# The first y_b product issued inside attention's last round

## The chip, the cores and the metric

The kernel runs on one core of a Trainium2 chip. The metric is the device time of one execution in microseconds (us); three executions of a kernel give a median. A core has TensorE (PE, with its weight loads shown apart as PEld), VectorE (DVE), ScalarE (ACT), GpSimd (POOL), and SyncE (SP), which here only issues DMA transfers, in order. Each engine works through its own list of instructions in order; between engines there are semaphores.

## The reference, cut to what matters

The reference is one decoder block on 2048 positions and a width of 1024, in float32. One projection feeds two branches: dilated band attention (three head groups of eight heads, 64 wide) and a gated linear recurrence (RG-LRU). The two results are gated, added, projected and normalised:

```python
attn = attn.reshape(B, S, ATTN_OUT_WIDTH).astype(dt) * jax.nn.silu(g_attn)
y_a = attn @ w_attn_proj[l]
...
y_b = (h * jax.nn.silu(g_lru)) @ w_lru_proj[l]
gates = jax.nn.sigmoid(gate_logits).reshape(B, S, N_BRANCHES, D)
merged = gates[:, :, 0] * y_a + gates[:, :, 1] * y_b
out = merged @ w_out[l] + b_out[l]
x = layer_norm(DEEPNORM_ALPHA * x + out, ln_gain[l], ln_bias[l])
```

The product for y_b needs the recurrence alone, not the attention. It is computed transposed: 8 blocks of 128 output channels by 4 chunks of 512 positions, 32 blocks in all, each a sum over 8 blocks of 128 channels.

## The kernel before, in words

The program has three stages in a row. The projection and the recurrence come first (the `q` products of line 602). Attention follows, and then the back end: the y_b jobs, the combination of the head groups, the y_a jobs and the output projection with its normalisation. Every float32 operand of a large product is split in a high part and a rest, so that one product is three matmuls (high by high, high by rest, rest by high).

**Attention** is written as a software pipeline of 48 units of work, `i` from 0 to 47, with three more turns of the loop to empty it. In turn `i` the loop issues the scores of `i` (line 981, into PSUM tiles with the tag `s`, four of them, one bank each), masks and maximum of `i` on DVE (line 988), exponentials of `i` and `i - 1` on ACT (line 996), the transposes of the exponentials of `i - 1` in two halves (`turn(i - 1, 0)` and `turn(i - 1, 1)`, line 1006, 16 small matmuls each in these units, into PSUM tiles with the tag `t`), the copies of those transposes to SBUF (`bring`, lines 1019 and 1021), and the product with the values of `i - 2` (`values`, line 1034, which also takes a `t` tile, `o`). Three turns later `leave` copies `o` to SBUF on DVE (lines 1043 to 1047), and a turn after that SP stores it to DRAM. There are four `t` tiles, used in rotation: a half of a unit's transposes takes two, a value product takes one. Turn 48 issues the transposes of unit 47 and the values of unit 46; turn 49 the values of unit 47.

The operands of y_b are made during attention: `prep_wl` loads and splits two 128-column weight blocks at a time (`wl`), `load_h` the recurrence's output of the first chunk (`h`), split by POOL. After the loop `prep_wl(4)` to `prep_wl(7)` put eight more weight loads on SP's queue, behind the last stores of attention's outputs (`o_scr<-ot`) and of its statistics (`st_scr<-sta`).

**The y_b jobs**, `yb_job(n)` for n from 0 to 31, follow. Each takes one of four PSUM tiles with the tag `y`, issues 24 matmuls (lines 1281 to 1283), and has DVE multiply the result with the gate `gB` (line 1287), which `load_gb` has fetched from DRAM; SP stores it to `yb_scr` (line 1288). Job n asks for the gate of job n + 2. The pools of attention are closed before those of the back end are opened, so the `y` tiles lie in banks that were `s` tiles. Job 1 also reads attention's statistics back (`stats`), from which DVE and ACT work out the groups' weights (lines 1184 to 1200); a transpose inside job 6 (line 1208) uses them. Splits of the weights for jobs 4 to 7 stand between these on ACT (line 1072) and DVE (line 1073).

The order of each engine's list is the order in which the code below is written; nothing moves it later.

Of the kernel before, what the change touches and what calls it, by code (L numbers as in the profile page):

```python
# [8 lines left out]
F32 = mybir.dt.float32  # L9
F32R = mybir.dt.float32r  # L10
AF = mybir.ActivationFunctionType
ALU = mybir.AluOpType
# [3 lines left out]
P = 128  # L16
S = 2048
D = 1024
KT = 8
NCH = 4  # L20
CH = 512
# [10 lines left out]
def hybrid_block_kernel(ctx: ExitStack, tc: tile.TileContext, a: dict, out: bass.AP):  # L32
    nc = tc.nc
    sp, act, dve, pool, pe = nc.sync, nc.scalar, nc.vector, nc.gpsimd, nc.tensor
# [12 lines left out]
    mg_scr = dram.tile([2 * D, S], F32, name="mg_scr")  # L47
    yb_scr = dram.tile([D, S], F32, name="yb_scr")
# [40 lines left out]
    now = {"n": 0}  # L89
# [831 lines left out]
    n = len(where)  # L921
# [61 lines left out]
    def peak(i, j, h):  # L983
        u, q = divmod(i, 4)
        lo = first(i, j)
        if h == 0:
            st["p", i, j] = p_p.tile([P, 2, 256], F32, tag="p", name=f"p{i}{j}")
        dve.tensor_tensor_reduce(out=st["p", i, j][:, h, lo:256], in0=st["s", i, j // 2][h][:, j % 2, lo:256],  # L988
                                 in1=mask[:, lo:256], scale=1.0, scalar=3e38, op0=ALU.add, op1=ALU.min,
                                 accum_out=sta[u][:, 4 * q + j, h:h + 1])  # L990
# [32 lines left out]
    def values(i):  # L1023
        u, q = divmod(i, 4)
        g, hp = unit(u)
        V = VT[g, hp // 2]
        o = st["o", i] = aps.tile([P, 4, P], F32, tag="t", name=f"o{i}", bufs=4)
        for j in range(4):
            ptb = st["b", i, j // 2]
            n = 4 * q + j  # L1030
            for x in range(first(i, j) // P, 2):
                for h, hs in enumerate(HALF):
                    v0 = P * (hp % 2) + 64 * h
                    pe.matmul(o[hs, j, :], V[:, n if x else prev(g, n), v0:v0 + 64], ptb[:, j % 2, x, h, :],  # L1034
                              start=(x == first(i, j) // P), stop=(x == 1))
# [48 lines left out]
    def load_h(c, k, lag):  # L1084
# [3 lines left out]
        sp.dma_start(flat(t[:, 1]), hb_scr[k * P:(k + 1) * P, c * CH:(c + 1) * CH])  # L1088
        later(lag, lambda: split(t[:, 0], t[:, 1], dve if c else pool))

    NG = 48
    for fn in v_parts(2, 0) + third:
        fn()
# [2 lines left out]
    for i in range(NG + 3):  # L1096
        u = i // 4
        on, turns = i < NG, 0 < i <= NG
        run(late)
        if i in VORD:  # L1100
            loads += v_parts(*VORD[i])
        if i % 4 == 0 and 1 <= u <= 9:
            loads += unit_parts(u + 2)
        for _ in range(2):
            if loads:
                loads.pop(0)()
        if on:
            scores(i)
        if i > 2:
            leave(i - 3)  # L1110
        if turns:
            expo(i - 1, 2, 1)
            expo(i - 1, 3, 0)
            expo(i - 1, 3, 1)
        if on:
            peak(i, 0, 0)
            expo(i, 0, 0)
            for j, h in ((0, 1), (1, 0), (1, 1)):
                peak(i, j, h)
        if turns:  # L1120
            turn(i - 1, 0)
            bring(i - 1, 0, 0, act)
            bring(i - 1, 0, 1, dve)
        if on:
            for j, h in ((0, 1), (1, 0), (1, 1)):
                expo(i, j, h)
            peak(i, 2, 0)
            peak(i, 2, 1)
        if turns:
            turn(i - 1, 1)  # L1130
            light = unit((i - 1) // 4)[0] == 2 or i % 3 == 0
            bring(i - 1, 1, 0, dve if light else act)
        if on:
            peak(i, 3, 0)
            peak(i, 3, 1)
            expo(i, 2, 0)
        if turns:
            bring(i - 1, 1, 1, dve)
        if i > 1 and i - 2 < NG:
            values(i - 2)  # L1140
        if i in (40, 41):
            prep_wl(i - 40, 2)
        if 42 <= i < 46:
            load_h(0, 2 * (i - 42), 2)
            load_h(0, 2 * (i - 42) + 1, 2)
        if i in (46, 47):
            prep_wl(i - 44, 2)
        now["n"] += 1
# [118 lines left out]
    def load_gb(n):  # L1267
        c, f = divmod(n, 8)
        GB[n] = gt(f"gB{n}")
        sp.dma_start(GB[n], mg_scr[D + f * P:D + (f + 1) * P, c * CH:(c + 1) * CH])  # L1270

    def yb_job(n):
        c, f = divmod(n, 8)
        cs = slice(c * CH, (c + 1) * CH)
        run(late)
        if n + 2 < 32:
            load_gb(n + 2)
        yb = fp.tile([P, CH], F32, tag="y", name=f"yb{c}{f}", bufs=4)
        for k in range(8):
            xx = HH[c, k]  # L1280
            pe.matmul(yb, WL[f][:, 0, k], xx[:, 0], start=(k == 0), stop=False)  # L1281
            pe.matmul(yb, WL[f][:, 0, k], xx[:, 1], start=False, stop=False)  # L1282
            pe.matmul(yb, WL[f][:, 1, k], xx[:, 0], start=False, stop=(k == 7))  # L1283
            if k == 3:
                run(pe_late)
        gb = GB.pop(n)
        dve.scalar_tensor_tensor(out=gb, in0=gb, scalar=1.0, in1=yb, op0=ALU.add, op1=ALU.mult)
        later(1, lambda: sp.dma_start(yb_scr[f * P:(f + 1) * P, cs], gb))
        now["n"] += 1
# [7 lines left out]
        sp.dma_start(YG[i][0], mg_scr[f * P:(f + 1) * P, cs])  # L1297
        sp.dma_start(YG[i][1], yb_scr[f * P:(f + 1) * P, cs])

    load_gb(0)  # L1300
    load_gb(1)
    for n in range(32):
        c, f = divmod(n, 8)
# [223 lines left out]
```

## Time and profile before

| | us |
|---|---|
| median of 3 executions (lowest to highest) | 2129.75 (2129.43 to 2129.99) |
| the profiled execution's own time | 2130.19 |
| its span, first to last instruction | 2128.4 |
| turn 48 of attention begins on PE (first transposes of unit 47) | at 1663.35 |
| first y_b matmul | at 1669.35 |
| second y_b job begins | at 1674.94 |

The granted TensorE clock is 0.998 of full speed over the span. PE is busy for 98% of the span. The times in the last three rows are counted from the span's start. A row of the timeline gives the start, the duration, the engine, the line, the operation with its output and input, and in square brackets how long the engine had stood idle before it and who ended that idle time. PE's end of a matmul is modelled, so neighbouring matmuls overlap in the rows; what one costs in a stream is the distance between starts.

### The profile page before, as it was taken

The numbers are of one execution on the slowest core, as the hardware profiler recorded it, in microseconds if no ns is written. First come the engines' busy times: TensorE is split into PE (matmuls) and PEld (weight loads), VectorE is DVE, ScalarE is ACT, GpSimd is POOL, SyncE is SP. The second block draws the span as 40 slices with busy tenths as digits, with TensorE's granted clock in tenths as the row PEclk, the third lists the DMA queues.
The fourth block names the chain that finished last, engine by engine and source line by source line (L and its number), as shares of the span: only waits on it lengthen the run. The fifth ranks groups of instructions, "written<-read, shape, count | busy, mean of one in ns | idle before, by whom it ended". The sixth has DMA issues, their size and how long they took to land.

```text
span 2128.4 us, 35700 instructions
## 1 busy us (share of the span) xinstructions
PE 2093.8 (98%) x12016; PEld 1745.9 (82%) x12016; DVE 1672.6 (79%) x3193; ACT 1078.8 (51%) x2284; POOL 457.6 (22%) x397
## 2 busy tenths in 40 slices
PE   8999999999999999999999999999999999999998
PEld 7888888888878888888888888888888888878887
DVE  8888889799789867787787887886999645476667
ACT  6355445357356566546557656657999411121100
POOL 1001011011011002121221221223535444332120
PEclk9999999999999999999999999999999999999999
DMA  9987997988988876677778788879998688874431
GB/s 273 275 267 218 290 261 238 272 265 250 278 271 257 305 220 196 221 226 219 249 251 270 262 256 254 256 227 383 289 310 262 210 280 281 290 246 162 163 109 70
DMA packets 348263, 525.72 MB, mean 247 GB/s; under 512 B 123568, under 2 KB 156336, under 8 KB 344240
## 3 DMA queue, kind: packets, MB, share of 16 engines
q1 hardware_dynamic: 330368, 491.64, 71.3%
q0 software_dynamic: 10080, 18.35, 5.4%
q10 hardware_dynamic: 7632, 13.44, 1.7%
q8 instruction: 96, 1.57, 0.3%
q14 instruction: 87, 0.71, 0.1%
HBM read 318.18 MB, written 190.45 MB: 239 GB/s over the span
## 4 chain that ended last, share of the span: by engine, by line
PE 60%; ACT 6%; DMA 3%; DVE 2%; issue 1%; SPq 1%; POOL 0%; DVEq 0%; ACTq 0%
PE q L602 37%; ACT p L996 4%; PE z L1393 3%; PE z L1391 3%; PE z L1392 3%; PE yb L1281 2%; PE yb L1282 2%; PE yb L1283 2%; PE o L1034 1%; ACT ptb L1019 1%; PE ya L1361 1%; PE ya L1360 1%; PE ya L1359 1%; PE s L981 1%; DMA yb_scr<-gB 1%; DVE p L988 1%
## 5 line engine op out<-in xcount | busy, mean ns | idle before, releaser
L602 PE MATMUL q<-xT,hS 128*128 128x512 f32 x1680 | 518.8, 390 | 0.0
L602 PE MATMUL q<-xT,l 128*128 128x512 f32 x1120 | 436.0, 389 | 0.0
L602 PE MATMUL q<-xB,hA 128*128 128x512 f32 x1248 | 387.3, 392 | 5.7 <-ACT xB L207 5.7
L602 PEld LDWEIGHTS q<-xT,hS 128*128 128x128 f32 x1680 | 314.1, 188 | 64.3
L602 PE MATMUL q<-xB,l 128*128 128x512 f32 x904 | 352.9, 390 | 0.5 <-DMA l<-wl_scr 0.4
L602 PEld LDWEIGHTS q<-xB,hA 128*128 128x128 f32 x1248 | 234.1, 188 | 54.4 <-ACT xB L207 5.7
L602 PEld LDWEIGHTS q<-xT,l 128*128 128x128 f32 x1120 | 210.2, 188 | 44.3
L602 PEld LDWEIGHTS q<-xB,l 128*128 128x128 f32 x904 | 170.1, 188 | 37.5 <-DMA l<-wl_scr 0.8
L264 ACT ACTIVATE hA<-wA 128x512 fp32r<-128x512 f32 x218 | 135.5, 623 | 82.1 <-DMA wA<-in_w_in_dram 44.0
L602 PE MATMUL q<-xB,hS 128*128 128x512 f32 x560 | 173.5, 391 | 2.2 <-DVE v L219 2.2
L996 ACT ACTIVATE p<-p,sta 128x256 f32<-128x256 f32 (+1 forms) x384 | 172.2, 455 | 5.9 <-DVE sta L988 5.2
L602 PE MATMUL q<-xT,hA 128*128 128x512 f32 x560 | 172.8, 390 | 0.0
L237 POOL DMA_DIRECT2D wS<-in_w_in_dram x70 | 61.1, 935 | 477.6 <-DMA wS<-in_w_in_dram 120.0
L264 ACT ACTIVATE hS<-S 128x512 fp32r<-128x512 f32 x175 | 109.0, 623 | 87.9 <-DVE S L219 48.4
L219 POOL TENSOR_TENSOR S<-S,wA 128x512 f32<-128x512 f32 x35 | 45.6, 1303 | 445.8 <-DVE S L219 319.1
L602 PEld LDWEIGHTS q<-xB,hS 128*128 128x128 f32 x560 | 104.2, 188 | 23.8 <-issue 2.6
L602 PEld LDWEIGHTS q<-xT,hA 128*128 128x128 f32 x560 | 104.7, 188 | 21.9 <-issue 0.4
L988 DVE CUSTOM_DVE_ANT_0 p<-s,mask 128x256 f32<-128x256 f32 (+1 forms) x384 | 118.8, 360 | 4.6 <-PE s L981 3.6
L1393 PE MATMUL z<-wo,ml 128*128 128x512 f32 (+1 forms) x264 | 101.1, 383 | 0.8 <-DVE ml L1378 0.8
L1391 PE MATMUL z<-wo,mh 128*128 128x512 f32 (+1 forms) x264 | 101.1, 383 | 0.1
L1392 PE MATMUL z<-wo,mh 128*128 128x512 f32 (+1 forms) x264 | 101.0, 383 | 0.0
L1281 PE MATMUL yb<-h,wl 128*128 128x512 f32 x256 | 100.3, 392 | 0.0
(199 smaller groups left out, 4182.1 us busy)
## 6 DMA issues: line engine op xcount, KB each, us to landing
wA<-in_w_in_dram SPq DMA_DIRECT2D x253, 256.0 KB, 5.0
wl_scr<-l SPq DMA_DIRECT2D x105, 512.0 KB, 5.3
l<-wl_scr SPq DMA_DIRECT2D x105, 512.0 KB, 4.8
sw<-y SPq DMA_DIRECT2D x384, 64.0 KB, 3.1
wS<-in_w_in_dram SPq DMA_DIRECT2D x70, 256.0 KB, 4.8
wS<-in_w_in_dram POOLq DMA_DIRECT2D x70, 256.0 KB, 6.4
qh_scr<-hi SPq DMA_DIRECT2D x48, 256.0 KB, 5.8
v_scr<-vs SPq DMA_DIRECT2D x48, 256.0 KB, 4.4
```

The source lines that it names most:

```text
L219: eng.tensor_tensor(out=out, in0=in0, in1=in1, op=op)
L237: pool.dma_start(t, w_part(s, x), accum_op=ALU.add)
L264: act.activation(h, r, AF.Copy)
L602: pe.matmul(bank, w[:, ks], x[:, kk, xx], start=(first and i == 0), stop=(last and i == 11))
L988: dve.tensor_tensor_reduce(out=st["p", i, j][:, h, lo:256], in0=st["s", i, j // 2][h][:, j % 2, lo:256], in1=mask[:, lo:256], scale=1.0, s ...
L996: act.activation(p, p, AF.Exp, scale=-1.0, bias=s[:, h:h + 1], accum_out=s[:, 2 + h:3 + h])
L1281: pe.matmul(yb, WL[f][:, 0, k], xx[:, 0], start=(k == 0), stop=False)
L1282: pe.matmul(yb, WL[f][:, 0, k], xx[:, 1], start=False, stop=False)
L1283: pe.matmul(yb, WL[f][:, 1, k], xx[:, 0], start=False, stop=(k == 7))
L1391: pe.matmul(z, mh[:, k], w[:, 0, hs], start=(k == 0), stop=False)
L1392: pe.matmul(z, mh[:, k], w[:, 1, hs], start=False, stop=False)
L1393: pe.matmul(z, ml[:, k], w[:, 0, hs], start=False, stop=(k == 7))
```

## The change

The 24 matmuls of the first y_b job move into turns 48 and 49 of the attention loop, with a fourth user of the tag `s` as their PSUM tile. The values of unit 46 move ahead of the second half of the transposes of unit 47. The gate for this job is fetched in turn 48, into a tile of the pool `p_p` that held exponentials, and the multiplication and the store to `yb_scr` are issued in turn 50. `yb_job(0)` keeps what else it did (`run(late)`, the load of the gate for job 2) and returns; `load_gb(0)` goes.

```diff
+    Y0 = {}
+
+    def yb_first(k0, k1):
+
+        if k0 == 0:
+            Y0["b"] = aps.tile([P, 2, 256], F32, tag="s", name="yb00", bufs=4).rearrange("p a b -> p (a b)")
+        for k in range(k0, k1):
+            xx = HH[0, k]
+            pe.matmul(Y0["b"], WL[0][:, 0, k], xx[:, 0], start=(k == 0), stop=False)
+            pe.matmul(Y0["b"], WL[0][:, 0, k], xx[:, 1], start=False, stop=False)
+            pe.matmul(Y0["b"], WL[0][:, 1, k], xx[:, 0], start=False, stop=(k == 7))
+
+    def yb_first_gate():
+        g = Y0["g"] = p_p.tile([P, 2, 256], F32, tag="p", name="gB0").rearrange("p a b -> p (a b)")
+        sp.dma_start(g, mg_scr[D:D + P, 0:CH])
+
+    def yb_first_out():
+        g = Y0["g"]
+        dve.scalar_tensor_tensor(out=g, in0=g, scalar=1.0, in1=Y0["b"], op0=ALU.add, op1=ALU.mult)
+        sp.dma_start(yb_scr[0:P, 0:CH], g)
+
...
+        if i == NG:
+            values(i - 2)
+            yb_first(0, 2)
         if turns:
             turn(i - 1, 1)
...
             bring(i - 1, 1, 1, dve)
-        if i > 1 and i - 2 < NG:
+        if i == NG:
+            yb_first_gate()
+            yb_first(2, 4)
+        if i > 1 and i != NG and i - 2 < NG:
             values(i - 2)
+        if i == NG + 1:
+            yb_first(4, 8)
+        if i == NG + 2:
+            yb_first_out()
...
         if n + 2 < 32:
             load_gb(n + 2)
+        if n == 0:
+            now["n"] += 1
+            return
...
-    load_gb(0)
     load_gb(1)
```

What this makes of the engines' lists is shown at two places. The first is PE at the end of attention. In the names `pt470` and `pt471` are the two halves of unit 47's transposes (a last digit tells the two tiles of a half), `o46` and `o47` the value products, `yb00` and `yb01` the first two y_b jobs; what a row waits for stands in brackets, and a line of dots stands for rows of the same kind. Before:

```order
L1006 MATMUL pt4701_19249<-ident_180,p471_19165 128x64
L1006 MATMUL pt4710_19269<-ident_180,p472_19192 128x64 [waits DVE_49,Activation_49]
...
L1006 MATMUL pt4711_19270<-ident_180,p473_19215 128x64
L1034 MATMUL o46_19290<-ptb460_19186,V11_16983 64x128 [waits DVE_49]
L1034 MATMUL o46_19290<-ptb461_19213,V11_16983 64x128 x8
L1034 MATMUL o47_19313<-ptb470_19266,V11_16983 64x128 [waits Activation_49]
L1034 MATMUL o47_19313<-ptb471_19287,V11_16983 64x128 [waits DVE_49]
L1281 MATMUL yb00_19375<-h00_18738,wl0_18551 128x512 [waits Pool_49]
...
L1281 MATMUL yb01_19416<-h00_18738,wl0_18551 128x512
```

Changed, at the same place:

```order
L1006 MATMUL pt4701_19249<-ident_180,p471_19165 128x64
L1034 MATMUL o46_19269<-ptb460_19186,V11_16983 64x128 [waits DVE_49]
L1034 MATMUL o46_19269<-ptb461_19213,V11_16983 64x128 x8
L1099 MATMUL yb00_19286<-h00_18738,wl0_18551 128x512 [waits Pool_49]
...
L1006 MATMUL pt4710_19293<-ident_180,p472_19192 128x64 [waits DVE_49,Activation_49]
...
L1099 MATMUL yb00_19286<-h00_18738,wl0_18551 128x512 [waits Pool_49]
...
L1034 MATMUL o47_19328<-ptb470_19266,V11_16983 64x128 [waits Activation_49]
L1034 MATMUL o47_19328<-ptb471_19311,V11_16983 64x128 [waits DVE_49]
L1099 MATMUL yb00_19286<-h04_18923,wl0_18551 128x512 [waits Pool_49]
...
L1315 MATMUL yb01_19416<-h00_18738,wl0_18551 128x512 [waits DVE_49]
```

The 24 matmuls of `yb00` now stand in three groups of 6, 6 and 12, the value product of unit 46 stands ahead of `pt471`, and the first matmul of `yb01` has a wait for DVE that it had not before: `yb01` lies in the same PSUM bank as the new `yb00`, and the DVE instruction that it waits for is the multiplication of line 1109, which reads that bank.

The second place is SP's list of transfers from the last outputs of attention on (`o_scr<-ot`: unit 44 first). Before:

```order
L1049 DMA o_scr13_65<-ot11_18838 128x512 [waits DMAHW3_49,DVE_49]
L1049 DMA o_scr13_65<-ot11_18838 128x512 [waits DMAHW4_49,DVE_49]
L1061 DMA st_scr_70<-sta11_18837 512x1x4 [waits DMAHW5_49,Activation_49]
...
L1081 DMA wl4_19337<-wf_scr4_157 128x512 [waits DMAHW1_49]
L1081 DMA wl4_19337<-wf_scr5_158 128x512 [waits DMAHW3_49]
...
L1270 DMA gB0_19366<-mg_scr_73 128x512 [waits DMAHW1_49,PE_49]
L1270 DMA gB1_19368<-mg_scr_73 128x512 [waits DMAHW2_49]
...
L1170 DMA stats_19401<-st_scr_70 128x16x48 [waits DMAHW6_49,PE_49]
...
L1288 DMA yb_scr_74<-gB0_19366 128x512 [waits DMAHW1_49,DVE_49]
```

Changed:

```order
L1105 DMA gB0_19314<-mg_scr_73 128x512 [waits DMAHW2_49,PE_49,Activation_49]
L1049 DMA o_scr13_65<-ot11_18838 128x512 [waits DMAHW3_49,DVE_49]
L1049 DMA o_scr13_65<-ot11_18838 128x512 [waits DMAHW4_49,DVE_49]
L1110 DMA yb_scr_74<-gB0_19314 128x512 [waits DMAHW5_49,DVE_49]
L1049 DMA o_scr13_65<-ot11_18838 128x512 [waits DMAHW6_49]
L1061 DMA st_scr_70<-sta11_18837 512x1x4 [waits DMAHW7_49]
...
L1081 DMA wl4_19366<-wf_scr4_157 128x512 [waits DMAHW3_49]
L1081 DMA wl4_19366<-wf_scr5_158 128x512 [waits DMAHW5_49]
...
L1301 DMA gB1_19395<-mg_scr_73 128x512 [waits DMAHW3_49,PE_49]
...
L1201 DMA stats_19402<-st_scr_70 128x16x48 [waits DMAHW7_49,PE_49]
```

The gate of the first job moved ahead of attention's last three output stores, and the store of the first job's result moved from behind the `stats` load to a place ahead of the last output store, the statistics and the eight weight loads. That store waits for the multiplication of line 1109.

## The prediction

> **What bounds the kernel now.** I read the page's busy shares first, then the table by stage, then what PE waited for, and then the timeline row by row where the change sits. The first three, in that order:
>
> ```profile
> PE 2093.8 (98%) x12016; PEld 1745.9 (82%) x12016; DVE 1672.6 (79%) x3193; ACT 1078.8 (51%) x2284; POOL 457.6 (22%) x397
> ...
> 1663.35:1665.71 2.36, 2.01 (x34) 1.49 (x33) 1.50 (x3) 2.36 (x10) 1.37 (x3) 1.00 0.81 301
> 1669.35:1674.94 5.59, 5.59 (x26) 4.62 (x25) 0.69 (x1) 0.00 (x0) 4.70 (x3) 1.00 0.45 100
> 1669.35:1856.90 187.55, 187.55 (x834) 154.68 (x833) 91.62 (x145) 32.47 (x58) 69.98 (x51) 1.00 0.85 274
> ...
> PE o L1034 <- ACT ptb L1019: 0.6, 1, 0.6
> PE pt L1006 <- ACT p L996: 0.4, 2, 0.2
> ```
>
> The window rows give length, then busy time of PE, PEld, DVE, ACT and POOL. PE is the bound of the kernel, and in the 187.55 us of y_b jobs it is busy for 187.55: whatever delays or advances the first y_b jobs on PE moves the end by as much. The two wait rows are all that PE waited for a data producer between 1660 and 1860 us. So the only gap this change can fill is turn 48, 1663.35 to 1665.71, where PEld is busy for 1.49 of 2.36 us and ACT for all of it. Row by row:
>
> ```profile
> 1654.76 1.23 PEld L1006 LDWEIGHTS pt<-ident,p 64*128 64x128 f32 x32
> 1663.35 0.69 PEld L1006 LDWEIGHTS pt<-ident,p 64*128 64x128 f32 x17 [0.17 <-issue]
> 1663.47 0.69 DVE L1045 COPY ot<-o 128x512 f32<-128x512 f32 x1
> 1664.21 0.44 PEld L1006 LDWEIGHTS pt<-ident,p 64*128 64x128 f32 x7 [0.18 <-DVE ot L1045]
> 1664.73 0.50 ACT L996 ACTIVATE p<-p,sta 128x256 f32<-128x256 f32 x1
> 1664.88 0.14 PEld L1006 LDWEIGHTS pt<-ident,p 64*128 64x128 f32 x2 [0.23 <-ACT p L996]
> 1665.38 0.26 PEld L1006 LDWEIGHTS pt<-ident,p 64*128 64x128 f32 x6 [0.35 <-ACT p L996]
> 1665.71 3.47 PEld L1034 LDWEIGHTS o<-ptb,V 128*64 128x64 f32 x64
> 1669.35 0.19 PEld L1281 LDWEIGHTS yb<-h,wl 128*128 128x128 f32 x1 [0.17 <-issue]
> 1669.69 0.39 PE L1282 MATMUL yb<-h,wl 128*128 128x512 f32 x1
> 1674.72 0.39 PE L1283 MATMUL yb<-h,wl 128*128 128x512 f32 x1
> 1674.94 0.39 PE L1281 MATMUL yb<-h,wl 128*128 128x512 f32 x1
> ```
>
> The 32 transposes of a turn take 1.23 us when nothing holds them (first row) and 2.36 here, because the second half waits for a PSUM tile (DVE) and then, one after another, for the last three exponentials on ACT. About 1.1 us is to be had, at most. From 1669.35 to 1674.94 is the first y_b job: the first of its matmuls is followed after 0.34 us, the others every 5.25/23 = 0.228 us.
>
> **The change part by part.** I count PE's time from 1663.35 to the start of the second y_b job, which is 11.59 us before.
>
> Moved work, at its old price: 32 transposes 1.23, both value products 3.47, 24 y_b matmuls 24 x 0.228 = 5.47; together 10.17. Their inputs are there: the values of unit 46 need DVE's copy before the `ot` copy of 1663.47; the second half of the transposes comes some 3.3 us later than before (values 1.74, six matmuls 1.37, their switches), at about 1667.5, when the last exponential, begun at 1664.73, is long done. The second half of the values of unit 47 needs two DVE copies behind those transposes (1.29 us for the pair below), which six y_b matmuls (1.37) and the first half of the values (0.87) cover. The operands of the y_b job were split by 1660.1:
>
> ```profile
> 1658.80 1.29 POOL L1073 TENSOR_TENSOR h<-h 128x512 fp32r<-128x512 f32 x1
> 1665.87 1.29 DVE L1021 COPY ptb<-pt 128x512 f32<-128x512 f32 x2 [0.96 <-PE pt L1006]
> 1454.66 0.39 PE L602 MATMUL q<-xB,l 128*128 128x512 f32 x1
> 1454.97 0.32 PE L981 MATMUL s<-B,A 64*128 64x128 f32 x1
> ```
>
> Added: switches between kinds of matmul. The rows name the shape of the array (64\*128 for transposes, 128\*64 for values, 128\*128 for y_b). Values to y_b costs 0.17 idle and 0.34 - 0.23 = 0.11 for the late second matmul, 0.28 in all (1669.35 row); transposes to values 0.07 (1665.38 + 0.26 to 1665.71); full array to 64 rows 0.31 - 0.23 = 0.08 (1454.66 to 1454.97). Before there is one switch of 0.07 and one of 0.28. Changed there are one of 0.07, two of 0.28, and three that no row shows in this place (y_b to transposes, transposes to y_b, y_b to values), each between 0.07 and 0.28; I take 0.15, nearer to the two cheap rows, whose pairs resemble them more. That is 0.07 + 0.56 + 0.45 = 1.08.
>
> The Trainium skill speaks against breaking a stream up: "TensorEngine Tiling (Array Packing)", Key Properties, says that changing the tiling mode drains TensorE. The rows agree in one direction only, since the cheap switches show 0.07 and 0.08. By the rule in its strict form the three unknown switches would cost 0.28 each, and the sum below would be 0.4 higher; that is the third rival.
>
> So without anything else the second y_b job would begin 10.17 + 1.08 = 11.25 us after 1663.35, 0.34 sooner than before (0.58 sooner with the cheap switches, nothing sooner with the dear ones).
>
> **The wait that comes with it.** The second job lies in the bank of the first, so its first matmul waits until DVE has multiplied the first job's result out of it. Before, the next job had another bank. What this costs can be read from a place where a job's end, the next job and DVE's multiplication stand side by side:
>
> ```profile
> 1714.01 0.39 PE L1283 MATMUL yb<-h,wl 128*128 128x512 f32 x1
> 1714.24 0.39 PE L1281 MATMUL yb<-h,wl 128*128 128x512 f32 x1
> 1714.44 0.69 DVE L1287 SCALAR_TENSOR_TENSOR gB<-gB,yb 128x512 f32<-128x512 f32 x1 [1.32 <-PE yb L1283]
> ...
> DMA to landing us min/median/max: 2.4/5.5/6.6
> ```
>
> The next job began at 1714.24; DVE read from 1714.44 to 1715.13, and PE answers DVE's end 0.05 us later (copy over at 1664.16, weights at 1664.21). The next job would have begun at 1715.18: 0.94 late. A start after idle costs perhaps the 0.11 of the second matmul again: between 0.94 and 1.05, and I take 1.05. The gate itself is early: it is issued right behind the first store of the next fence, at about 1660, and 6.6 us is the longest landing of a gate, so it is there by 1667. Queued behind the waiting matmul is all of PE's work, so the wait counts in full. Net: 1.05 - 0.34 = **+0.7 us**, with +0.36 and +1.10 at the ends of the terms.
>
> **The queue behind.** The store of the first job's result now heads SP's queue ahead of the last attention store, the statistics, the weights for jobs 4 to 7 and the read of `stats`.
>
> ```profile
> 1659.62 10.89 SPq L1049 DMA_DIRECT2D o_scr<-ot  x4
> 1673.26 4.17 SPq L1081 DMA_DIRECT2D wl<-wf_scr  x8
> 1677.71 0.91 SPq L1270 DMA_DIRECT2D gB<-mg_scr  x2
> 1681.26 0.37 SPq L1170 DMA_DIRECT2D stats<-st_scr  x1
> 1669.47 0.69 DVE L1045 COPY ot<-o 128x512 f32<-128x512 f32 x1 [1.05 <-PE o L1034]
> 1683.33 0.69 DVE L1287 SCALAR_TENSOR_TENSOR gB<-gB,yb 128x512 f32<-128x512 f32 x1 [13.17 <-DMA gB<-mg_scr]
> 1688.98 0.29 DVE L1184 TENSOR_TENSOR wmx<-stats 128x128 f32<-128x128 f32 x1 [2.99 <-DMA stats<-st_scr]
> 1691.45 1.29 DVE L1073 TENSOR_TENSOR wl<-wl 128x512 fp32r<-128x512 f32 x2 [1.11 <-ACT wl L1072]
> 1699.28 0.56 DVE L1200 TENSOR_TENSOR whl<-wgt,whl 128x384 fp32r<-128x384 f32 x1 [0.67 <-ACT whl L1199]
> 1696.70 0.39 PE L1281 MATMUL yb<-h,wl 128*128 128x512 f32 x1
> 1697.16 0.39 PE L1283 MATMUL yb<-h,wl 128*128 128x512 f32 x1
> 1704.87 0.60 PE L1208 MATMUL wtp<-ident,whl 128*128 128x128 f32 x4
> yb_scr<-gB SPq DMA_DIRECT2D x3, 256.0 KB, 4.6
> ```
>
> Before, that part of the queue was released when DVE's last `ot` copy ended, 1669.47 + 0.69 = 1670.16; now by the multiplication, which ends about 1674.60 + 0.20 + 0.69 = 1675.5 (1674.60 is the second job's start without the wait, the rest as at 1714). One store more in front and one gate less cancel (0.91/2 = 0.46 us of issue each), so the `stats` read is some 5.3 us later, and one weight load, which waits for the first job's store to land (4.6), may add 0.3. Gone in exchange is DVE's wait of 13.17 us for the first gate, which covered nothing on PE. Three users are near. The weights of the sixth job hang on `stats` by the order of ACT and DVE: their first half is split by 1691.45 + 0.65 = 1692.1, now 1697.4 to 1697.7; PE wants it at 1697.16 + 0.7 = 1697.9. The transposed group weights are ready at 1699.84, now 1705.1 to 1705.4; PE wants them at 1704.87 + 0.7 = 1705.6. Both just hold, by 0.2 to 0.5 us, so I put this edit at nothing; it is the thinnest cover in the sum. The third, the multiplications that free banks for jobs 5 and later, has several us left.
>
> **The rivals.** A measurement of this kernel tells no difference below about 0.2% (4.3 us), so all sizes here are small.
>
> - **Late loads** (slower than forecast and than before). The same two waits hold, and the loads come more than 0.5 us later than shifted. The point of decision is the sixth job's third matmul. Its price: the landing of a gate spreads from 5.5 to 6.6, so 1.1 late, less 0.2 to 0.5 of cover, is 0.6 to 0.9, once; what PE loses there it need not lose again at 1705. Total +1.3 to +1.6, or 2131.2. For more than 0.2% the whole chain would have to come some 4 us later still. For it speaks that the burst of loads fills the DMA engines (the DMA column of the y_b row is 0.85); against it, that the burst is the same as before, a little shorter.
> - **The fill wins** (a little faster). If the bank's wait is shorter than its rows say, because DVE could begin before PE's modelled end, and the switches cost their least, the gain of 0.58 stands against some 0.4: 2129.6. For it: PE's ends are modelled. Against it: the pair of rows at 1714 shows DVE beginning after that end, and its 0.69 is measured.
> - **Dear switches**. Each of the three costs 0.28 as from values to y_b: 1.05 + 0.05 = +1.1, or 2130.85.
> - **It does not do what it says.** The stalls stay, because the values of unit 46 find no free bank: then the gain of about 1.1 is missing and the sum is +1.8, or 2131.55. The list speaks against it: the value product now waits for a copy that ended before 1663.47.
>
> **How the numbers follow.** The profiled execution took 2130.19 us, 0.44 above the median of 2129.75; the difference of +0.7 is taken from its rows and put on the median: 2130.5. Chances: forecast 0.50 (own range 2130.1 to 2130.9), late loads 0.20, dear switches 0.12, the fill wins 0.13, does nothing 0.05. The range takes in the fill (2129.6 less the distance of the lowest run from the median, 0.3, and a little) and late loads with the highest terms (2129.75 + 1.10 + 0.9 + 0.3 = 2132.05, and a little more where two of the loads are late): 2129.1 to 2132.3. Faster by over 0.2% has 0.01: no row offers 4 us. Slower by over 0.2% has 0.04, all from late loads that pile up. Within 0.2%: 0.95.
>
> **What would show it.** Right: no idle time from ACT on PE in turn 48; the first matmul of the second job idle for about 0.95 us, released by DVE's multiplication of line 1109, its start near 1675.5 instead of 1674.94; the DVE wait of 13.17 us gone; the first weight load of the eight issued near 1679. Wrong: the second job starting before 1674.9 (the switches or the wait were overpriced), idle rows on PE at the sixth job or at the transposes of the group weights (late loads), or value products that wait in turn 48.

## The result, and the profile after

| | before | changed |
|---|---|---|
| median of 5 executions (lowest to highest), us | 2129.75 (2128.1 to 2132.1) | 2139.65 (2138.1 to 2142.04) |
| the profiled execution: its time, its span, us | 2130.19, 2128.4 | 2139.65, 2137.9 |

The ratio is 1.0047, with a 95% interval of 1.0036 to 1.0058: the change made the kernel slower by about half a per cent. The forecast was 2130.5 (2129.1 to 2132.3), with a chance of 0.04 for what happened.

The page of the changed kernel has the same instructions and nearly the same busy times as before (PE 2093.8 us there); most of the lost time is not work:

```profile
PE 2097.1 (98%) x12016; PEld 1745.0 (82%) x12016; DVE 1671.4 (78%) x3193; ACT 1079.3 (50%) x2284; POOL 456.5 (21%) x397
```

The table by stretch shows where it is. The three rows are turn 48 up to the second y_b job, from there to the first y_a matmul, and from there to the first matmul of the output projection (length, then busy time of PE, PEld, DVE, ACT and POOL, clock, DMA share, GB/s). First the kernel before, then the changed one:

```profile
1663.35:1674.94 11.59, 11.24 (x122) 9.57 (x121) 4.17 (x7) 2.46 (x10) 8.96 (x8) 1.00 0.42 122
1674.94:1857.10 182.16, 182.16 (x810) 150.23 (x809) 91.13 (x144) 32.67 (x58) 65.28 (x48) 1.00 0.87 279
1857.10:1878.90 21.80, 21.80 (x98) 17.97 (x97) 10.66 (x17) 4.77 (x9) 8.23 (x5) 1.00 0.95 311
```

```profile
1668.63:1680.71 12.08, 11.34 (x122) 8.94 (x120) 4.77 (x8) 2.46 (x10) 7.61 (x8) 1.00 0.31 108
1680.71:1863.98 183.27, 183.03 (x809) 150.29 (x810) 86.24 (x140) 31.45 (x56) 65.39 (x49) 1.00 0.86 274
1863.98:1888.05 24.07, 22.31 (x98) 17.84 (x97) 12.63 (x20) 5.88 (x10) 8.27 (x5) 1.00 0.94 312
```

So the 9.5 us between the spans are: 5.3 before turn 48 (1668.63 against 1663.35), 0.5 in the turn, 1.1 in the y_b jobs, 2.3 in the y_a jobs, and 0.4 behind. The lists of all engines are the same in both kernels up to the start of turn 48, so the first 5.3 needs another reason than the change; the experiments come back to it. Of the other 4 us, 2.6 stand in what PE waited for between 1660 and 1890 us, where the first and third row are new:

```profile
PE ya L1392 <- DVE gA L1397: 1.8, 2, 1.1
PE o L1034 <- ACT ptb L1019: 1.0, 2, 0.6
PE yb L1315 <- DVE gB L1109: 0.8, 1, 0.8
PE pt L1006 <- ACT p L996: 0.2, 1, 0.2
```

The kernel before has in this stretch, beside its waits for ACT, one wait alone, and that lies in the output projection:

```profile
PE z L1393 <- DVE ml L1378: 0.8, 1, 0.8
```

Turn 48 itself, on PE:

```profile
1668.63 0.77 PE L1006 MATMUL pt<-ident,p 64*128 64x64 f32 x16
1669.33 1.97 PE L1034 MATMUL o<-ptb,V 128*64 128x128 f32 x32
1671.23 0.50 PE L1099 MATMUL yb<-h,wl 128*128 128x512 f32 x1
...
1672.49 0.40 PE L1101 MATMUL yb<-h,wl 128*128 128x512 f32 x1
1672.81 0.71 PE L1006 MATMUL pt<-ident,p 64*128 64x64 f32 x16
1673.46 0.50 PE L1099 MATMUL yb<-h,wl 128*128 128x512 f32 x1
1673.79 0.39 PE L1100 MATMUL yb<-h,wl 128*128 128x512 f32 x1
...
1674.72 0.40 PE L1101 MATMUL yb<-h,wl 128*128 128x512 f32 x1
1675.05 1.97 PE L1034 MATMUL o<-ptb,V 128*64 128x128 f32 x32
1676.95 0.50 PE L1099 MATMUL yb<-h,wl 128*128 128x512 f32 x1
...
1679.58 0.39 PE L1101 MATMUL yb<-h,wl 128*128 128x512 f32 x1
1680.75 0.50 PE L1315 MATMUL yb<-h,wl 128*128 128x512 f32 x1 [0.78 <-DVE gB L1109]
1681.08 0.40 PE L1316 MATMUL yb<-h,wl 128*128 128x512 f32 x1
```

The waits for ACT at the transposes are filled, as the prediction had it. The last row but one is the bank's wait: the next matmul was due 0.23 after 1679.58 and came at 1680.75, 0.94 late. Turn 48 to the second job is 12.12 us by the matmul's own row (1680.75), against 11.59.

The two waits at y_a lie 200 us further on. SP's queue shows what links them to the change:

```profile
1669.47 6.38 SPq L1049 DMA_DIRECT2D o_scr<-ot  x2
1680.72 0.32 SPq L1110 DMA_DIRECT2D yb_scr<-gB  x1
...
1684.21 4.44 SPq L1081 DMA_DIRECT2D wl<-wf_scr  x8
...
1691.87 0.37 SPq L1201 DMA_DIRECT2D stats<-st_scr  x1
```

The first weight load left 3.5 us after the start of the second job (1684.21 against 1680.75); before, 1.7 us ahead of it (1673.26 against 1674.94). I call **lag** the time from the start of the second y_b job to the issue of the `stats` read: 11.1 us here, 6.3 before. At the end of the y_b stage the gates for y_a are late. DVE, and then PE behind it:

```profile
1877.67 0.69 DVE L1397 SCALAR_TENSOR_TENSOR gA<-gA,ya 128x512 f32<-128x512 f32 x1 [4.29 <-DMA gA<-mg_scr]
...
1881.67 0.69 DVE L1397 SCALAR_TENSOR_TENSOR gA<-gA,ya 128x512 f32<-128x512 f32 x1 [2.71 <-DMA gA<-mg_scr]
```

```profile
1878.41 0.50 PE L1392 MATMUL ya<-at,wa 128*128 128x512 f32 x1 [0.70 <-DVE gA L1397]
...
1882.50 0.47 PE L1392 MATMUL ya<-at,wa 128*128 128x512 f32 x1 [1.06 <-DVE gA L1397]
```

A y_a job needs a PSUM tile, DVE frees it by multiplying it with the gate, and the gate's load stands in SP's list behind everything that the held store delayed.

The 1.1 us of the y_b jobs lie for the most part at one place too small for the list of waits: the three products with the group weights (`bc`), 168 us after the second job's start. Each waits a little for DVE, and together they take 0.84 us longer. The first row is before, the second changed:

```profile
1842.76 0.86 PE L1223 MATMUL bc<-wT,sel 128*128 128x512 f32 x3
1848.77 1.70 PE L1254 MATMUL bc<-wT,sel 128*128 128x512 f32 x3
```

### The profile page after: what moved, and what is told of

It is laid out like the page before. It is cut to its first block, busy times and chain, and to the rows that moved or that the text cites. A ratio compares the mean times of both kernels' runs of the same rounds, so it can differ in the third digit from the quotient of the medians.

```text
span 2137.9 us, 35698 instructions
## 1 busy us (share of the span) xinstructions
PE 2097.1 (98%) x12016; PEld 1745.0 (82%) x12016; DVE 1671.4 (78%) x3193; ACT 1079.3 (50%) x2284; POOL 456.5 (21%) x397
## 4 chain that ended last, share of the span: by engine, by line
PE 54%; DMA 7%; ACT 6%; DVE 2%; SPq 1%; issue 1%; POOL 0%; DVEq 0%; ACTq 0%; POOLq 0%
PE q L602 37%; ACT p L996 4%; PE z L1426 2%; PE z L1425 2%; PE z L1424 2%; DMA yb_scr<-gB 2%; DMA at_scr<-oc 2%; PE o L1034 2%; ACT ptb L1019 1%; PE ya L1393 1%; PE ya L1394 1%; PE s L981 1%; PE ya L1392 1%; DVE p L988 1%; PE yb L1315 1%
## 5 line engine op out<-in xcount | busy, mean ns | idle before, releaser
L219 DVE TENSOR_TENSOR y<-y,cos 128x512 f32<-128x512 f32 x96 | 78.0, 819 | 25.6 <-DMA sw<-y 25.5
```

What stands on the lines that cost most here:

```text
L219: eng.tensor_tensor(out=out, in0=in0, in1=in1, op=op)
```

## The experiments

The theory after this (A): the store at the head of SP's queue delays all loads of the y_b stage, the queue does not catch up, and PE pays at the end of the stage. The letters of the rivals are used afresh in each of three batches, and in the third A is written A'. All runs in one table, by lag; "way" is from the start of the second y_b job to the first matmul of the output projection. Lag, turn and way come from one traced execution each; the ratio compares with executions of the kernel before from the same session:

| kernel | lag, us | turn 48 to second job, us | way, us | median, us | ratio to before (95%) |
|---|---|---|---|---|---|
| early | 3.1 | 11.59 | 203.9 | 2129.70 | 0.9997 (0.9988 to 1.0006) |
| before | 6.3 | 11.59 | 203.9 | 2129.45 to 2130.36 | 1 |
| best | 6.8 | 11.18 | 204.2 | 2128.95 | 0.9997 (0.9988 to 1.0006) |
| hold_ahead | 7.3 | 12.12 | 204.0 | 2129.57 | 0.9998 (0.9990 to 1.0007) |
| store | 7.4 | 12.11 | 204.0 | 2130.17 | 1.0000 (0.9991 to 1.0010) |
| both | 8.3 | 12.11 | 204.3 | 2130.80 | 0.9998 (0.9988 to 1.0009) |
| truebank | 9.4 | 11.17 | 207.5 | 2132.42 | 1.0011 (0.9999 to 1.0022) |
| again2 (changed) | 11.0 | 12.11 | 206.2 | 2135.75 | 1.0028 (1.0019 to 1.0037) |
| bank | 11.0 | 12.15 | 207.3 | 2135.40 | 1.0022 (1.0012 to 1.0032) |
| again (changed) | 11.1 | 12.11 | 208.1 | 2135.79 | 1.0020 (1.0010 to 1.0030) |
| changed, first | 11.1 | 12.12 | 207.3 | 2139.65 | 1.0047 (1.0036 to 1.0058) |
| behind | 12.0 | 12.12 | 209.4 | 2135.51 | 1.0021 (1.0012 to 1.0030) |
| delay | 12.1 | 11.59 | 211.3 | 2138.14 | 1.0039 (1.0026 to 1.0051) |
| dose | 16.9 | 11.19 | 213.8 | 2140.31 | 1.0048 (1.0035 to 1.0061) |

**again**: the changed kernel unchanged, beside the next three.

> The changed kernel once more, to see what of its loss comes back. In its first profile the turn that takes the new matmuls began 5.3 us later than before, ahead of any instruction that differs. Theory A (the loss is made behind that point: about 0.5 us by the bank's wait less the fill, 1 us in the y_b jobs, 2 us where y_a starts, all but the first by SP's queue; what lies ahead is scatter): the start of turn 48 moves by several us from profile to profile and on the mean is that of before, and the median is +4 us (0.2%). Rival B (something in the changed program slows the stages ahead of it): turn 48 begins at 1668 to 1669 us again and the median is +9 to +10 us.

Measured: 2135.79, ratio 1.0020; turn 48 began at 1660.36 in its trace, not at 1668.63. Over the fourteen traces that moment lies between 1660.36 and 1668.63, and the changed kernel alone has 1660.36, 1667.13 and 1668.63. So the 5.3 us ahead of the change were scatter in this trace, while a long way (208.1) came again.

**store**: the one store moves from SP's queue to ACT's.

```diff
-        sp.dma_start(yb_scr[0:P, 0:CH], g)
+        act.dma_start(yb_scr[0:P, 0:CH], g)
```

> The store of the first job's result is issued from ACT's queue instead of SP's; nothing else moves, so the bank's wait stays. The last attention store, the statistics and the eight weight loads are then released by the last copy of attention's output, about 3.5 to 4 us sooner than in the changed kernel. Theory A: the stalls at y_a and in the y_b jobs go, 2.5 to 3.5 us sooner than the changed kernel. Rival (bank's wait): no difference to the changed kernel beyond 0.5 us. Rival B: about 2 us at most, and still some 6 us behind the kernel before.

Measured: way 204.0, no wait of PE at y_a, time that of the kernel before. One row in a queue carried the loss; the bank's wait, still there, cannot be seen in the time.

**bank** and **both**: an attempt to give the second job another bank, without and with the store on ACT's queue.

```diff
         if n == 0:
+            fp.tile([P, CH], F32, tag="y", name="yskip", bufs=4)
             now["n"] += 1
             return
```

> One y tile is skipped in the first job, so the second job lies in another bank than the first and doesn't wait for the multiplication of line 1109. Theory A: 0.8 to 1.0 us sooner than the changed kernel at the start of the second job, but the end hardly moves (0 to 1 us), because the late loads behind the store still set the start of y_a. Rival (the bank's wait is what costs): the whole loss behind turn 48 goes, about 4 us.

> Both edits: the store from ACT's queue and the second job in another bank. Theory A: the loss is gone, within 1 us of the kernel before, the second job starting about 0.3 us sooner after the start of turn 48 than before (11.25 instead of 11.59). Rival B: still 5 us or more slower than before, with turn 48 late.

Both expectations suppose that the wait goes, and it did not: the tile that nothing used moved nothing, and both traces still show PE waiting 0.8 us for line 1109. So the two are no test of the bank, only a second pair of changed (way 207.3) and repaired (204.3) kernels.

**delay**: all 24 matmuls of the first job back in their old place, with a bank apart from the second's; SP's queue stays as the change has it.

```diff
         if i == NG:
-            values(i - 2)
-            yb_first(0, 2)
...
             yb_first_gate()
-            yb_first(2, 4)
-        if i > 1 and i != NG and i - 2 < NG:
+        if i > 1 and i - 2 < NG:
             values(i - 2)
         if i == NG + 1:
-            yb_first(4, 8)
+            yb_first(0, 8)
...
+    fp.tile([P, 4, P], F32, tag="ct", name="ctskip", bufs=1)
     load_gb(1)
```

> Order of the matmuls as in the kernel before (all 24 of the first y_b product behind both value products, its bank apart from the next job's), but SP's queue as in the changed kernel: the store of the first product's result stands ahead of the last attention store, the statistics and the eight weight loads. Theory A (the held queue is the cost): from the start of turn 48 to the second y_b job 11.5 to 11.7 us, as before; the first of the eight weight loads 5 to 6 us later after the start of turn 48 than before; from the second y_b job to the first product of the last stage 207 to 208 us instead of 204.0; time +3 to +4 us over the kernel before. Rival B (the loss comes with the moved matmuls: switches, the bank, values sooner): 204.0 to 204.5 us and no difference in time.

Measured: the turn is that of before (11.59), the way 211.3, and the kernel is slower by 1.0039. The held queue alone makes the whole loss, and more of it than expected. Where, is in the waits of PE, and behind it in the timelines of ACT, DVE and PE (one fence each):

```profile
1844.71 0.63 ACT L1072 ACTIVATE at<-at 128x512 fp32r<-128x512 f32 x1 [7.95 <-DMA at<-at_scr]
```

```profile
1845.37 0.69 DVE L1073 TENSOR_TENSOR at<-at 128x512 fp32r<-128x512 f32 x1 [4.40 <-ACT at L1072]
1845.98 1.88 DVE L1251 TENSOR_TENSOR oc<-oc,bc 128x512 f32<-128x512 f32 x3
```

```profile
1842.64 0.39 PE L1313 MATMUL yb<-h,wl 128*128 128x512 f32 x1
1846.72 1.99 PE L1250 MATMUL bc<-wT,sel 128*128 128x512 f32 x3 [3.69 <-DVE oc L1251]
1848.51 0.63 PE L1311 MATMUL yb<-h,wl 128*128 128x512 f32 x1
1848.93 0.63 PE L1312 MATMUL yb<-h,wl 128*128 128x512 f32 x1
```

A load of the combined attention (`at`) is late, ACT's split waits for it, DVE's half of the split waits for ACT, and behind it on DVE stand the multiplications that free the PSUM tiles for the next products with the group weights (`bc`). PE stands for 3.69 us, 168 us after the second job's start. Then its matmuls follow every 0.43 us instead of 0.228, because the granted clock (the third number from the end of a row of the table by stretch) had fallen:

```profile
1841.38:1846.58 5.20, 1.65 (x8) 1.03 (x6) 1.21 (x2) 1.87 (x4) 0.00 (x0) 0.85 1.04 397
1846.58:1849.98 3.40, 3.26 (x7) 2.25 (x8) 2.53 (x5) 0.84 (x2) 2.56 (x2) 0.50 0.68 238
1849.98:1853.38 3.40, 3.40 (x13) 2.69 (x12) 3.40 (x4) 0.00 (x0) 1.61 (x1) 0.73 0.88 201
```

**dose**: the second job, too, stands ahead, and the store of its result also heads SP's queue.

```diff
         if i == NG + 2:
             yb_first_out()
+            b1 = aps.tile([P, 2, 256], F32, tag="s", name="yb01", bufs=4).rearrange("p a b -> p (a b)")
+            g1 = p_p.tile([P, 2, 256], F32, tag="p", name="gB1").rearrange("p a b -> p (a b)")
+            sp.dma_start(g1, mg_scr[D + P:D + 2 * P, 0:CH])
+            ...
+            dve.scalar_tensor_tensor(out=g1, in0=g1, scalar=1.0, in1=b1, op0=ALU.add, op1=ALU.mult)
+            sp.dma_start(yb_scr[P:2 * P, 0:CH], g1)
...
-        if n == 0:
+        if n < 2:
...
-    load_gb(1)
```

> The changed kernel, with the queue held for one job more: the second y_b product, too, stands ahead (in its own bank), and the store of its result also heads SP's queue, so that the last attention store, the statistics and the weight loads are issued some 5 to 6 us later again, about 11 us later than before. Theory A, each us of holding costs about one us once a cover of 1 to 2 us is used up: from the second y_b job to the last stage 212 to 214 us (changed kernel 207.3), time +8 to +10 us over the kernel before. Rival C, the queue catches up over 31 jobs, or the loss is a fixed one of having a store there: 207 to 209 us, time +3 to +5.

Measured: lag 16.9, way 213.8, as A had it (212 to 214). That the number fits so well is in part luck. A priced the holding us for us, but 6.7 of the 9.8 us over the way of before come at the sixth job, 3.8 of them as a wait and most of the rest by a granted clock of 0.50 behind it. The price comes sooner now, at the place where the prediction had looked for it, the weights of the sixth job; the rest comes late again (0.7 at the `bc` products, 1.1 at y_a):

```profile
PE yb L1325 <- ACT wl L1072: 3.8, 1, 3.8
PE ya L1401 <- DVE gA L1406: 1.1, 1, 1.1
```

**behind**: the store stays on SP's queue, behind the eight weight loads.

```diff
-        sp.dma_start(yb_scr[0:P, 0:CH], g)
...
     for f in range(4, 8):
         prep_wl(f, f - 3)
+    sp.dma_start(yb_scr[0:P, 0:CH], Y0["g"])
     stB.close()
```

> The changed kernel with the store of the first product still on SP's queue, only moved behind the eight weight loads (still ahead of the gates and the read of the statistics). The store can go at about the time at which the weight loads have been issued, so nothing waits behind it. Theory A: 204.0 to 204.5 us from the second y_b job to the last stage, 12.0 to 12.2 us from turn 48 to the second y_b job (the bank's wait stays), time +0 to +0.7 us over the kernel before, as with the store on ACT's queue. If it was ACT's queue that helped there and not the place in SP's: 207 us and +3 to +4.

This expectation failed: lag 12.0, way 209.4, time +0.21%. It was not ACT's queue that had helped, though. SP's timeline has the weight loads gone in time and a new gap behind the store:

```profile
1672.81 4.22 SPq L1081 DMA_DIRECT2D wl<-wf_scr  x8
1677.50 0.32 SPq L1183 DMA_DIRECT2D yb_scr<-gB  x1
1678.12 0.37 SPq L1301 DMA_DIRECT2D gB<-mg_scr  x1
1683.22 0.98 SPq L1088 DMA_DIRECT2D h<-hb_scr  x2
```

The list of SP's waits names it: `SPq L1088 <- DMA yb_scr<-gB: 4.7, 1, 4.7`. The load of `h` waits for that store to land. Its buffer, of 16 KB a partition, is in a pool of the back end that is opened after the pool of the first gate's tile (2 KB) is closed. That it takes over the memory which the store still reads is my reading of the wait; no run shows the addresses. In `store`, where the same store left 4.7 us sooner after the second job's start, this load had no such wait. What holds the queue has changed, what a held queue costs has not.

**truebank**: the store on ACT's queue, and the `y` tiles begun one bank further by taking the back end's `ct` tile first, so that the second job lies apart from the first.

```diff
+    fp.tile([P, 4, P], F32, tag="ct", name="ctskip", bufs=1)
     load_gb(1)
     for n in range(32):
```

> The changed kernel with the store on ACT's queue and the second y_b job in another bank than the first, so that its first matmul waits for nothing (the first attempt at this left the bank as it was). Theory A with the prediction's terms: from turn 48 to the second y_b job 11.1 to 11.3 us (changed kernel 12.08, kernel before 11.59), from there 204.0 to 204.3 us, time 0.2 to 0.5 us under the kernel before, which the comparison can hardly tell from no change. If the breaks in the stream cost more than the rows said and the bank's wait less: 11.6 to 12.0 us, and no gain.

Measured: no wait, and 11.17 us from turn 48 to the second job. The bank's wait thus costs 12.12 - 11.17 = 0.95 us. But the way is 207.5, and the time no better than before. PE is now ahead by 0.9 us, the queue is not, and the lag becomes 9.4. Against `both` (8.3) that is 1.1 more at the start, but at the first gate of y_a 3.6 more (issued 186.65 against 183.01 us after the second job's start): here the lag grows on its way. The twelve executions lie in two groups, 2126.7 to 2129.5 (five) and 2132.0 to 2136.8 (seven). A kernel at the edge of its cover would do that, but only one execution, of the upper group, has a trace.

**hold_ahead**: everything of the change stays, the held store and the shared bank too; only the eight weight loads go ahead of it.

```diff
+        if i == NG:
+            for f in range(4, 8):
+                prep_wl(f, f + 9)
         if i > 2:
             leave(i - 3)
...
-    for f in range(4, 8):
-        prep_wl(f, f - 3)
     stB.close()
```

> The changed kernel with everything of it, the store at the head of SP's queue and the shared bank too; only the eight loads of the weights for jobs 4 to 7 are issued at the start of turn 48, ahead of the held store, instead of behind it. The eight runs so far give a lag for each kernel, from the start of the second y_b job to the issue of the read of the statistics: up to 8.3 us (kernel before 6.3) the way from the second y_b job to the last stage takes 204.0 to 204.3 us, from 9.4 on 207 and more. Theory A' (what counts is how far SP's queue lags behind PE when the y_b stage begins, since it never catches up there): the lag becomes 6 to 7 us although the hold is the same, the way 204.0 to 204.5 us, no wait of PE for the last products with the group weights or for gates of y_a; time +0.3 to +1 us over the kernel before. Rival D (the held store does harm by itself, by what it holds apart from the weights): 207 us, +3 to +5.

Measured: way 204.0, time 0.9998 of before. SP's timeline shows the store held as long as ever, with less behind it:

```profile
1659.05 6.87 SPq L1081 DMA_DIRECT2D wl<-wf_scr  x8
...
1666.49 3.11 SPq L1049 DMA_DIRECT2D o_scr<-ot  x2
1674.47 0.32 SPq L1110 DMA_DIRECT2D yb_scr<-gB  x1
...
1681.75 0.43 SPq L1202 DMA_DIRECT2D stats<-st_scr  x1
```

So the held store does no harm by itself; what counts is how late the loads behind it enter the stage.

**early**, **best** and **again2**: the same move of the weight loads in the kernel before; in the changed kernel with the store on ACT's queue and the bank apart; and the changed kernel again.

> The kernel before with only this move: the eight loads of the weights for jobs 4 to 7 issued at the start of turn 48, when the DMA engines have little to do. Theory A': the lag falls from 6.3 to about 2 us, the way from the second y_b job to the last stage stays 203.8 to 204.1 us (PE has no gap there to give), the profiled time stays within 0.5 us; over many executions the median falls by 0 to 1.5 us, because the executions that lie several us above the median (up to 2137) are in part such lags. Rival: the scatter is all from the stages ahead, and nothing changes.

> The changed kernel with all three repairs: the store on ACT's queue, the second y_b job in a bank of its own, the eight weight loads at the start of turn 48. Theory A': from turn 48 to the second y_b job 11.1 to 11.3 us (11.59 before), a lag of 5 to 6 us, the way on 203.8 to 204.3 us; time 0.2 to 1.5 us under the kernel before, without the upper half of executions that the kernel with two repairs had (2132 to 2137). If that upper half came from somewhere else: 2132 again.

> The changed kernel once more, beside the three above. Theory A': lag 11 us, from turn 48 to the second y_b job 12.1 us, the way on 207 to 208.5 us, PE waiting for the last products with the group weights or for the first gates of y_a; time +4 to +9 us over the kernel before.

Measured: `early` cuts the lag to 3.1 and gains nothing in the median: below a lag of 8 there is nothing left to gain. (Its eleven executions end at 2131.49, where three of 33 of the kernel before lie above 2133; too few to tell whether such executions are lags.) `best` has a short turn (11.18), a short lag (6.8, above the 5 to 6 expected) and the lowest median of all, but the 0.41 us that it gains in the turn cannot be told from no change in 2130. `again2` lies between before and the first result: way 206.2, just under the 207 to 208.5 expected, ratio 1.0028.

**Where the way's jump comes from.** The way jumps by 3 us between a lag of 8.3 and one of 9.4. The traces show why, in the moment at which the loads of the combined attention (`at`) leave SP, counted from the second job's start. In the six kernels with a way of 203.9 to 204.3 it is 149.8 to 157.6 us (156.7 before). In the others PE loses time at the `bc` products, and the more the later these loads leave (`delay` and `dose`, where the clock or a late PE changes the sum, are left out):

| | changed, first | again2 | truebank | bank | again | behind |
|---|---|---|---|---|---|---|
| `at` loads issued, us | 159.9 | 160.0 | 160.5 | 160.6 | 160.7 | 161.9 |
| lost at the `bc` products, us | 0.95 | 1.46 | 1.61 | 1.95 | 2.03 | 3.00 |

So the cover there ends at about 159 us, and from there a us late costs about a us. The rest of the way's loss in these six, 0.8 to 2.4 us, comes at the gates of y_a. The lag at the start sets this moment only roughly: of the 4.7 to 4.8 us that the changed kernel lags more than before, 3.2 to 4.0 are left at these loads. `store` and `both`, with lags 1.1 and 2.0 above that of before, issue them 1.1 us sooner and 0.4 us later than before, while `truebank`'s 3.1 has become 3.8. What makes the queue drift is not known.

**What stays open.** Three times the changed kernel was compared, with ratios of 1.0047, 1.0020 and 1.0028. Its traces explain +0.5 in the turn and +2.3 to +4.2 in the way, so 2.8 to 4.7 us; the two later medians lie 5.4 and 6.3 over those of before beside them, the first 9.9. Part of each is thus not explained, and most of it in the first, where all five executions took over 2138 us and the one with a trace has 5.3 us ahead of turn 48, with lists that are the same. Over the fourteen traces two things go with a late turn 48: all waits of PE ahead of it, 22.8 to 27.7 us, above all one of the `q` products for DVE (line 219, 0.3 to 4.8 us), and a granted clock of 0.50 for some 3.4 us near 590 or 1470 us, which is worth 1.7 us and stands in nine of the traces (twice in `dose`). The first trace of the changed kernel has 3.2 us more of such waits than that of the kernel before, and as much of the slow clock. What makes them scatter from execution to execution, and from session to session, was not found.

## Why the prediction was wrong, point by point

- **The turn** was right. 11.25 us were predicted without the bank's wait, 11.17 and 11.18 measured where it is gone. The three switches that no row had shown, taken at 0.15, cost, late second matmul included: transposes to y_b 0.14 (1672.81 to 1673.46, less 16 transposes at 1.23/32, and 0.10 in the second matmul's place), y_b to transposes 0.09 (1672.49 to 1672.81, less 0.23), y_b to values 0.10 (1674.72 to 1675.05, less 0.23). The dear switches (0.28 each) fell. The Trainium skill, "TensorEngine Tiling (Array Packing)", Key Properties, says that a change of tiling mode drains TensorE; each of these switches does show a cost, 0.09 to 0.14, but not the 0.28 at which the prediction had priced that rule in its strict form.
- **The wait that comes with it** was right: 0.94 to 1.05 predicted, with 1.05 taken. Measured are 0.94 at the row and 0.10 more for the late second matmul behind it (1680.75 to 1681.08); taking the wait away gave 0.95 up to the second job's start.
- **Does nothing** and **the fill wins** fell: no wait for ACT is left in turn 48, and the wait was not cheaper than its rows said. All of PE's own terms together give +0.5 up to the second job's start and +0.6 with its late second matmul, predicted +0.7.
- **The queue behind** is the step that failed: "so I put this edit at nothing". The delay itself was sized well: the first weight load was to leave near 1679 with turn 48 at 1663.35, and left at 1684.21 - 5.28 = 1678.93. The two users named for it, the sixth job's weights and the transposes of the group weights, did hold, as said. What was missing is everything after them. I priced a delay by the first users behind it and let it end there; it measured +3.4 us (207.3 against 203.9), some 1 us at the `bc` products, 168 us later, and some 2 us at the gates of y_a, 196 and 200 us later. In the other traces of the changed kernel the `bc` products take the larger share or as much (2.0 and 2.1 in `again`, 1.5 and 0.8 in `again2`).
- A hint of this stood in the trace of before. SP waits in its own list for its own stores, in the whole y_b stage: 28.9 us in seven waits and 25.9 in twelve, out of 182. The first fence is before, the second changed:

```profile
SPq L1217 <- DMA at_scr<-oc: 28.9, 7, 4.9
SPq L1270 <- DMA yb_scr<-gB: 25.9, 12, 3.6
```

```profile
SPq L1248 <- DMA at_scr<-oc: 29.4, 7, 5.5
SPq L1301 <- DMA yb_scr<-gB: 25.4, 12, 3.3
```

  Much of the list stands behind the landing of an earlier store, and the sums are the same with the queue late. Such a list makes up little of a late start: 3.2 to 4.0 of the 4.7 to 4.8 us are left at the `at` loads. That these waits are the reason is argued, not tested.
- **Late loads**, the rival with 0.20, had the right direction and the wrong place: "the point of decision is the sixth job's third matmul". Its sentence that for 0.2% the chain would have to come 4 us later still was wrong, since the covers further on were thinner than the 5.3 us that I had myself worked out. `dose`, 5.8 us later again, is the case that the rival described, and there the sixth job does wait (3.8, at its first matmul). In `delay` it loses 0.6.
- **A second delay was not counted**: the values of unit 47 end later now, and with them DVE's last `ot` copy and the last attention store. With the held store gone (`store`, `both`) the lag is still 1.1 to 2.0 us over before. That would put the repaired kernel without the bank's wait at the edge.
- **The range** took its width from three executions within 0.6 us. In the sessions that followed the kernel before ran from 2126.0 to 2137.3.

## What to carry to other kernels

Where an engine that issues transfers in order enters a long stage, price a wait at the head of its list by the whole stage: compare how far the list lags behind the bound engine at the start, find every cover up to the stage's end, and take the thinnest. Do not count on a list that waits for its own stores to land to catch up; here it kept 3.2 to 4.0 of 4.8 us, and the price showed up hundreds of instructions from the edit. What has no need to wait (here eight weight loads) belongs ahead of what has, and a store that waits for a late producer belongs at the end of the list or on another queue, with a look at whose memory it reads.

## What the runs showed of the hardware

An idle time of PE can cost twice. In `delay` PE stood for 3.69 us. The row of the table by stretch that holds this wait has a mean clock of 0.85 over its 5.20 us, and the next row 0.50. If the clock fell once, it fell at about 1845.0, 2.0 us after the end of PE's last matmul (1842.64 + 0.39). It was back at 1851.8, and until 1851.49 a matmul came every 0.43 us. The wait and the slow clock cost 6.5 of the 7.4 us by which the way is longer than before. In `dose` a wait of 3.84 did the same: the clock fell 2.4 us after the end of PE's last matmul, and it stayed at 0.50 for 6.8 us. In `behind` a wait of 2.00, at the same place as in `delay`, left the clock at 1.00. The Trainium skill, "TensorE: Matmul & The Clock Gate", Part 1, says that TensorE's clock halves after an idle window of about 3.4 us. The half agrees with these traces, but here the clock fell after 2.0 and 2.4 us of idle time. So a wait for a late load is cheap only while the clock holds, and these three waits do not say where that ends.
